# Convolution taps moved into idle stretches of VectorE, and a token scale folded into the scaling of q and k

## The chip, the cores and the metric

The kernel runs on one core of a Trainium2 chip. The metric is the device time of one execution in microseconds (us). A core has five engines that the profile names so: PE (TensorE, matmuls; its weight loads are shown as PEld), DVE (VectorE), ACT (ScalarE), POOL (GpSimd) and SP (SyncE, which here issues most of the DMAs). Each engine works through its own instructions in order and waits on semaphores for the others.

## What is computed

One layer of a hybrid encoder, with 1024 tokens of 1024 channels, all float32. The parts that matter here are the first half:

```python
h = rms_norm(x, norm1_g)
a, gate, q, k, v = split(h @ w_in)            # 512 columns each
u = a * sigmoid(gate)                         # GLU
y = depthwise_conv(u, dw_kernel) + dw_bias    # 31 taps along the tokens, for each channel
conv_out = silu(layer_norm(y))
q, k = rms_norm(q, per head), rms_norm(k, per head)    # 8 heads of 64
attn_out = neighbourhood_attention(q, k, v, rpb)       # 8 x 16 window on a 16 x 64 grid
x = x + concat(conv_out, attn_out) @ w_out
```

Then follows a SwiGLU feed-forward block of width 2816 with its own norm and residual.

## The kernel before, in words

**Matmuls.** Each float32 operand is split into a high and a low part, and each product is made of three matmuls (`mac`, lines 112 to 114). The norm's gain is applied to the transposed input, and the token scale `r1` (1 over the root mean square of a token) only after the projection, to its result in PSUM. PSUM has four banks for accumulators (`mm`), two for transposes (`tp`) and one double bank (`cv`).

**The projection stage.** One PE step is one 128-token tile of k, q or v, or one part of a GLU product, 24 matmuls of 512 columns. PE goes through: four tiles of k; the GLU of channel group 0; four tiles of k; the GLU of groups 1 to 3 (for each group two token halves `h`, for each half first the gate, part 0, then the value, part 1); eight tiles of q; eight tiles of v. Score tiles of the attention are put between the last tiles of v: score 0, v tile 6, score 1, v tile 7. Then comes the attention loop, then output projection, norm and feed-forward.

**What a step does beside PE.** `step` defers the work on a step's result by one step: it runs the callback of the step before, then one side tap (`side`). Programs are in written order; no scheduler changes it.

- `head_post` (k and q): ACT squares z by head and takes the root (`head_sq`, the result is d, line 375); DVE pumps two taps; `head_scale` takes the reciprocal (L380), multiplies it with the token scale (L381) and scales z from PSUM by it, for each head of 64 columns (L383); one more tap; the transposition on PE (`head_T`, L390) is woven in at the end of the PE step after the next, and ACT copies it to qT or kT (L395, L397).
- `gate`: DVE multiplies the accumulator with the row of token scales (L443), ACT takes the sigmoid (L444), DVE multiplies with the row again (L445), then three taps.
- `val`: DVE multiplies the accumulator with the gate into u (L451), then three taps. After the second half, u of the channel group is complete.
- v: ACT scales it and stores it by DMA; four taps are pumped.

**The convolution.** `conv_taps` is a stream of 25 VectorE operations for each of the four channel groups: a start (L314), 23 taps (L319, `acc += w * u`, u in SBUF, acc in the double PSUM bank `cv`) and an add (L324) of the seven side taps, which ACT (L341, L344) and POOL (L345) compute apart in `pa`. `pump(n)` issues the next n operations of the stream. When the stream needs a group whose u is not complete, a pump issues nothing and its turn is lost. Before score 0 is evaluated, `pump(200)` issues all that is left.

**Score evaluation.** For each score tile DVE adds the bias and finds the maximum (L624), and ACT takes the exponential (L626). The bank of a score tile is free for PE once L624 has read it.

## Time and profile before

| | before |
|---|---|
| median of 3 runs | 1070.03 us (1069.66 to 1070.52) |
| the profiled execution | 1070.39 us |
| its span, first to last instruction | 1068.6 us |
| mean granted clock of PE | 0.995 of full speed |
| DVE, ACT, POOL busy | 704.9, 451.3, 383.2 us |
| PE busy from 145 to 225 us, of 80 | 80.00 us |
| PE busy from 225 to 246 us, of 21 | 16.39 us, mean granted clock 0.84 |
| PE busy from 246 to 318 us, of 72 | 71.39 us |
| taps L319 | 92, 117.5 us |

Times in the rows of the profile are us from the start of the span unless they are marked as ns. A timeline row has start, length, engine, line, operation, out<-in, shape and count, and in brackets the idle time of the engine before it with what ended that. Lengths of successive operations can overlap a little, so the distance between two starts is what one costs in a row of them. Names such as z, zn or cv are tiles, with buffer numbers left out.

### The profile page before, as it was taken

What the parts mean: (1) busy time and instruction counts of PE and PEld (TensorE: products, weight loads), DVE (VectorE), ACT (ScalarE), POOL (GpSimd) and SP (SyncE); (2) the same over time, 40 slices, a digit from 0 to 9 for tenths busy, and PEclk for the clock granted to TensorE, in tenths of its full rate; (3) what the DMA queues carried; (4) which work ended last, traced back from release to release, by engine and by line L of the source; (5) the groups of instructions that cost most, each with busy time, mean ns of one, the idle gap of its engine ahead of it and who ended that gap; (6) DMA issues with size and microseconds to landing.
All of it is one profiled execution on the core that took longest, in us unless ns stands there. A gap on an engine that the chain in (4) does not pass through costs nothing.

```text
span 1068.6 us, 14069 instructions
## 1 busy us (share of the span) xinstructions
PE 1048.0 (98%) x5068; PEld 849.4 (79%) x5068; DVE 704.9 (66%) x1071; ACT 451.3 (42%) x987; POOL 383.2 (36%) x301
## 2 busy tenths in 40 slices
PE   7999999989999999999999999999999999999997
PEld 6788888866667888788888888888888888888886
DVE  6778997885775347766556465564655567858873
ACT  6455357725775424542322323223232344433441
POOL 0136665513562301435444554445544300002310
PEclk9999999999999999999999999999999999999999
DMA  9426781244413422132322322333232597633641
GB/s 336 158 51 221 225 251 40 75 150 137 152 62 131 164 80 82 37 107 90 128 98 84 134 99 89 109 107 109 81 129 79 179 333 276 207 98 116 216 131 41
DMA packets 68245, 144.06 MB, mean 135 GB/s; under 512 B 12496, under 2 KB 21200, under 8 KB 67536
## 3 DMA queue, kind: packets, MB, share of 16 engines
q1 hardware_dynamic: 66336, 139.95, 38.8%
q10 hardware_dynamic: 1840, 3.22, 0.9%
q8 instruction: 40, 0.66, 0.3%
q14 instruction: 29, 0.24, 0.1%
HBM read 103.99 MB, written 44.76 MB: 139 GB/s over the span
## 4 chain that ended last, share of the span: by engine, by line
PE 89%; DVE 6%; issue 1%; ACT 1%; DMA 1%; POOL 0%; SPq 0%; DVEq 0%; POOLq 0%; ACTq 0%
PE B L113 5%; PE B L114 5%; PE B L112 5%; PE D L114 4%; PE D L112 4%; PE D L113 4%; PE A L112 3%; PE A L114 3%; PE A L113 3%; DVE cv L319 3%; PE gl L114 3%; PE gl L112 3%; PE gl L113 3%; PE z L112 2%; PE z L113 2%; PE z L114 2%
## 5 line engine op out<-in xcount | busy, mean ns | idle before, releaser
L319 DVE SCALAR_TENSOR_TENSOR cv<-u,par,cv 128x1009 f32<-128x1009 f32 (+14 forms) x92 | 117.5, 1277 | 2.5
L345 POOL TENSOR_TENSOR pa<-pa,pr 128x1022 f32<-128x1022 f32 (+5 forms) x24 | 57.5, 2398 | 51.3 <-ACT pr L344 42.8
L104 ACT CAST op<-sr 128x512 fp32r<-128x512 f32 x77 | 47.7, 619 | 51.2 <-PE B2d L114 23.3
L108 DVE TENSOR_TENSOR op<-sr,op 128x512 fp32r<-128x512 f32 x77 | 57.6, 748 | 15.9 <-ACT op L104 15.8
L1036 DVE TENSOR_TENSOR g<-B,g 128x512 f32<-128x512 f32 x22 | 15.2, 691 | 79.0 <-PE B L114 79.0
L1208 POOL TENSOR_TENSOR ou<-ou,resm 128x512 f32<-128x512 f32 x8 | 13.2, 1662 | 142.9 <-DMA resm<-xd 142.9
L1045 ACT ACTIVATE D<-D 128x512 f32<-128x512 f32 x22 | 12.8, 582 | 113.1 <-DVE D L1044 113.1
L1031 DVE TENSOR_TENSOR u<-B,g 128x512 f32<-128x512 f32 x22 | 15.2, 690 | 62.5 <-PE B L114 62.5
L104 ACT CAST op<-wd 128x512 fp32r<-128x512 f32 x66 | 40.9, 619 | 31.6 <-DVE wd L1123 18.3
L108 DVE TENSOR_TENSOR op<-wd,op 128x512 fp32r<-128x512 f32 x66 | 51.7, 783 | 2.4 <-ACT op L104 0.9
L633 POOL TENSOR_SCALAR e<-e,rs 128x288 f32<-128x288 f32 (+1 forms) x64 | 34.2, 548 | 52.8 <-DVE rs L631 42.3
L889 DVE TENSOR_TENSOR ts<-gu,ts 128x512 f32<-128x512 f32 x44 | 51.0, 1159 | 0.8
L1034 ACT ACTIVATE A<-A 128x512 f32<-128x512 f32 x20 | 11.6, 582 | 76.3 <-PE A L114 76.3
L626 ACT ACTIVATE e<-e,mx 128x288 f32<-128x288 f32 (+1 forms) x64 | 36.2, 568 | 11.4 <-DVE mx L624 11.4
L624 DVE CUSTOM_DVE_ANT_0 e<-s,tab 128x288 f32<-128x288 f32 (+1 forms) x64 | 29.9, 504 | 6.7 <-PE s L611 6.4
L889 DVE TENSOR_TENSOR ts<-gu 128x512 f32<-128x512 f32 x22 | 33.5, 1524 | 0.0
L611 PE MATMUL s<-kT,qT 64*128 64x288 f32 (+1 forms) x128 | 28.1, 499 | 4.6 <-DVE mx L624 4.6
L642 PEld LDWEIGHTS p<-ident,e 128*96 128x96 f32 (+1 forms) x192 | 20.1, 133 | 15.0 <-issue 10.4
L372 ACT ACTIVATE sq<-z,r 128x64 f32<-128x64 f32 x96 | 28.6, 334 | 2.2 <-PE z L114 2.2
L642 PE MATMUL p<-ident,e 128*96 128x128 f32 (+1 forms) x192 | 27.6, 280 | 0.6 <-DVE pT L647 0.6
L658 PE MATMUL o<-pT,vw 96*64 96x128 f32 (+1 forms) x384 | 28.0, 281 | 0.0
L344 ACT ACTIVATE pr<-u,par 128x1022 f32<-128x1022 f32 (+5 forms) x24 | 27.0, 1137 | 1.6 <-ACT vs L403 1.6
(1039 smaller groups left out, 3455.0 us busy)
## 6 DMA issues: line engine op xcount, KB each, us to landing
gu<-in_gu SPq DMA_DIRECT2D x44, 512.0 KB
sr<-sd SPq DMA_DIRECT2D x77, 256.0 KB
sd<-sd SPq DMA_DIRECT2D x22, 512.0 KB
wd<-in_wd SPq DMA_DIRECT2D x44, 256.0 KB
sd<-g SPq DMA_DIRECT2D x33, 256.0 KB
x<-in_x SPq DMA_DIRECT2D x16, 512.0 KB
xd<-x SPq DMA_DIRECT2D x8, 512.0 KB
resm<-xd SPq DMA_DIRECT2D x16, 256.0 KB
```

The lines of the kernel that those rows point to most:

```text
L104: act.copy(hi, src)
L108: eng.tensor_tensor(*[w[..., sl] for w in (lo, src, hi.bitcast(F32))], OP.subtract)
L112: pe.matmul(acc, lh, rh, start=start, stop=False, skip_group_check=True)
L113: pe.matmul(acc, lh, rl, start=False, stop=False, skip_group_check=True)
L114: pe.matmul(acc, ll, rh, start=False, stop=stop, skip_group_check=True)
L319: dve.scalar_tensor_tensor(acc[:, o], uc[:, i], dwk[:, c, t:t + 1], acc[:, o], OP.mult, OP.add)
L345: pool.tensor_tensor(pa[:, o], pa[:, o], pr[:, o], OP.add)
L624: dve.tensor_tensor_reduce(out=e[:, hh], in0=ss[hh], in1=tab[rh, cb][2 * hp + hh], scale=-1.0, scalar=3.0e38, op0=OP.add, op1=OP.min, accu ...
L626: act.activation(e[:, hh], e[:, hh], AF.Exp, bias=mx, scale=-1.0, accum_out=rs[:, hh:hh + 1])
L633: pool.tensor_scalar(es[i][:, hh], es[i][:, hh], rs[:, hh:hh + 1], 1.0, op0=OP.mult, op1=OP.mult)
L642: pe.transpose(pt[:m, g * P:(g + 1) * P], es[i][:, hh, g * m:(g + 1) * m], ident)
L889: dve.tensor_tensor(o, l, r, OP.subtract)
```

## The change

In `head_scale` the separate product of the reciprocal and the token scale goes; one VectorE operation with a per-partition scalar (the token scale) and a broadcast operand (the reciprocal) scales z from PSUM. Before `head_scale`, tile 5 of k pumps three taps more and tile 1 of q two more. In `gate`, one of the three taps (for the first half of group 1, two of then four) is pumped between the two products with the row.

```diff
     def head_scale(n, t, z, sd):
         r = SM(f"r{n}{t}")
         dve.reciprocal(r, sd)
-        dve.tensor_scalar(r, r, r1[:, t:t + 1], None, op0=OP.mult)
         zn = ST(f"zn{n}{t}")
-        dve.tensor_tensor(zn.rearrange("p (h d) -> p h d", d=HD), z.rearrange("p (h d) -> p h d", d=HD),
-                          r[:, :, None].to_broadcast([P, NH, HD]), OP.mult)
+        dve.scalar_tensor_tensor(zn.rearrange("p (h d) -> p h d", d=HD), z.rearrange("p (h d) -> p h d", d=HD),
+                                 r1[:, t:t + 1], r[:, :, None].to_broadcast([P, NH, HD]), OP.mult, OP.mult)
         return zn
...
     def head_post(n, t, z):
         def f(n_taps):
             sd = head_sq(n, t, z)
-            pump(2)
+            pump(2 + {(1, 5): 3, (0, 1): 2}.get((n, t), 0))
             zn = head_scale(n, t, z, sd)
             pump(1)
...
             dve.tensor_tensor(sg, acc, row, OP.mult)
             act.activation(sg, sg, AF.Sigmoid)
+            pump(2 if (c, h) == (1, 0) else 1)
             dve.tensor_tensor(sg, sg, row, OP.mult)
-            pump(n_taps - 1)
+            pump(n_taps - 2)
```

Here n is 1 for k and 0 for q, t the tile, and n_taps is 4.

## The prediction

> **What bounds the kernel now.** I read the page first. PE is busy for 98% of the span, so only what makes PE wait or run slowly can move the end. The waits of PE come next (engine, line, what it waited for: us in total, times, longest):

> ```profile
> PE 1048.0 (98%) x5068; PEld 849.4 (79%) x5068; DVE 704.9 (66%) x1071; ACT 451.3 (42%) x987; POOL 383.2 (36%) x301
> ...
> PE z L112 <- ACT wk0h L104: 6.5, 1, 6.5
> PE s L611 <- DVE mx L624: 4.6, 1, 4.6
> ```

> The first wait is the start of the kernel, which the change doesn't touch. The second is the only other one above 1 us. PE's timeline around it (start, length, ...):

> ```profile
> 225.27 0.76 PE L611 MATMUL s<-kT,qT 64*128 64x288 f32 x4
> 225.95 0.50 PE L112 MATMUL z<-w20h,hT 128*128 128x512 f32 x1
> ...
> 231.63 0.75 PE L611 MATMUL s<-kT,qT 64*128 64x288 f32 x2
> 237.00 1.32 PE L611 MATMUL s<-kT,qT 64*128 64x288 f32 x2 [4.61 <-DVE mx L624]
> 238.25 0.79 PE L112 MATMUL z<-w20h,hT 128*128 128x512 f32 x1
> ...
> 246.17 0.76 PE L611 MATMUL s<-kT,qT 64*128 64x288 f32 x4
> ```

> Two score tiles took 225.95 - 225.27 = 0.68 us at full pace, so one takes 0.34, and the second tile of score 1 could have started at 231.63 + 0.34 = 231.97. It started at 237.00: **5.03 us lost**. It needs the PSUM bank of the first tile of score 0, and VectorE frees that bank when L624 has read it.

> There is a second loss behind the first. z(6) and its lead-in took 231.63 - 225.95 = 5.68 us, but one score tile and z(7) took 246.17 - 237.00 = 9.17 us instead of 0.34 + 5.68 = 6.02: **3.15 us lost**. The stages view says why (stretch, its length, busy time of PE, PEld, DVE, ACT, POOL, then PE's granted clock, DMA share, GB/s):

> ```profile
> 236.00:237.00 1.00, 0.01 (x1) 0.01 (x1) 1.00 (x4) 0.00 (x0) 0.00 (x0) 0.63 0.00 0
> 237.00:238.00 1.00, 1.00 (x2) 0.49 (x2) 0.32 (x2) 0.96 (x4) 0.00 (x0) 0.50 0.00 0
> ...
> 242.00:243.00 1.00, 1.00 (x4) 0.81 (x3) 0.00 (x0) 0.00 (x0) 0.00 (x0) 0.50 0.00 0
> 243.00:244.00 1.00, 1.00 (x5) 0.77 (x5) 0.00 (x0) 0.00 (x0) 0.00 (x0) 0.96 0.00 0
> ...
> 32.00:33.00 1.00, 0.35 (x2) 0.20 (x2) 0.41 (x1) 0.56 (x1) 0.75 (x1) 1.00 1.00 401
> ...
> 248.00:249.00 1.00, 0.40 (x4) 0.02 (x1) 0.56 (x1) 1.00 (x4) 0.00 (x0) 1.00 0.53 199
> ```

> The granted clock fell to half late in the wait (0.63 in its last microsecond) and stayed there until about 243.1: six microseconds of matmuls at half speed cost three. The last two rows are PE's short pauses, 0.65 and 0.60 us of idle time, and the clock stayed at 1.00 in both.

> What VectorE did before it could read the score:

> ```profile
> 201.22 0.20 DVE L380 RECIPROCAL r<-d 128x8 f32<-128x8 f32 x1 [0.86 <-ACT d L375]
> 201.46 0.23 DVE L381 TENSOR_SCALAR r<-r,r 128x8 f32<-128x8 f32 x1
> 201.79 0.69 DVE L383 TENSOR_TENSOR zn<-z,r 128x512 f32<-128x512 f32 x1
> 202.40 1.21 DVE L324 TENSOR_TENSOR u<-cv,pa 128x1024 f32<-128x1024 f32 x1
> 203.65 1.35 DVE L314 TENSOR_SCALAR cv<-u,par 128x1024 f32<-128x1024 f32 x1
> 205.03 30.21 DVE L319 SCALAR_TENSOR_TENSOR cv<-u,par,cv 128x1009 f32<-128x1009 f32 x23
> 235.34 1.22 DVE L324 TENSOR_TENSOR u<-cv,pa 128x1024 f32<-128x1024 f32 x1
> 236.49 0.45 DVE L624 CUSTOM_DVE_ANT_0 e<-s,tab 128x288 f32<-128x288 f32 x1
> ```

> From 201.22 to 236.49 VectorE never waits. It is the convolution of the last channel group, all 25 of its operations, that the score stands behind. A tap costs (235.34 - 205.03) / 23 = 1.318 us. This tail's start is set by L380, which waited for the last q head's d, so it is PE and ACT, not VectorE, that set when the tail begins. Each operation taken out of the tail therefore moves 236.49.

> **The taps.** The holes into which they go (in brackets the idle time before each):

> ```profile
> 76.56 0.20 DVE L380 RECIPROCAL r<-d 128x8 f32<-128x8 f32 x1 [5.08 <-ACT d L375]
> ...
> 93.56 1.30 DVE L445 TENSOR_TENSOR sg<-sg,rb 128x512 f32<-128x512 f32 x1 [2.11 <-ACT sg L444]
> ...
> 104.39 0.69 DVE L445 TENSOR_TENSOR sg<-sg,rb 128x512 f32<-128x512 f32 x1 [0.70 <-ACT sg L444]
> ...
> 165.69 0.20 DVE L380 RECIPROCAL r<-d 128x8 f32<-128x8 f32 x1 [2.59 <-ACT d L375]
> ```

> Head k5 gets three taps more, 3 x 1.318 = 3.95 into 5.08. Head q1 gets two, 2.64 into 2.59. Gate (1,0) gets one more; the other gates only move one of their three into the hole. That makes six. But a pump does nothing when the next channel group isn't ready, and this costs three of them. Before, group 0 had done 24 of its 25 operations when val (1,1) completed u[1]. After, the four extra taps of k5 and gate (1,0) finish group 0 inside val (1,0), and the three pumps of gate (1,1) find nothing. So at val (1,1) the stream is ahead by one, and with q1's two by **three operations**; the instruction order of the changed program has this too: after the last zn stand 22 taps and one L324.

> The tail loses one L324, the L314 and one tap: (203.65 - 202.40) + (205.03 - 203.65) + 1.318 = 3.95 us.

> Nothing on the way should stop for the fillings. The holes of the gates end with ACT's sigmoid, so the gates get shorter, not longer: 0.70 of idle time becomes part of a tap. In q1 the 0.05 by which two taps exceed the hole is covered by the shorter gates before it. Behind a late head_scale stand only head_T and, on ACT, the next head's squares. SP's queue isn't changed; ACT and POOL have the same instructions in the same order. Two adds move up, and each needs POOL's sum of the side taps:

> ```profile
> 94.71 4.86 POOL L345 TENSOR_TENSOR pa<-pa,pr 128x1018 f32<-128x1018 f32 x2 [0.40 <-ACT pr L344]
> ...
> 184.59 2.39 POOL L345 TENSOR_TENSOR pa<-pa,pr 128x1017 f32<-128x1017 f32 x1 [1.16 <-ACT pr L344]
> ```

> Group 0's add moves from 109.40 to about 100.7 (gate (1,0) ends as before at 94.8, then two taps, one product of 0.6, two taps); POOL ends at 99.57, one microsecond before. If that is missed, VectorE waits a little where three pumps are empty anyway. Group 2's add moves to about 196.2; POOL ends at 186.98.

> **The fused scaling.** In each of 16 heads L381 goes and L383 becomes a two-operation form with z in PSUM and the broadcast r in SBUF. That form with these operands is not in the trace. The nearest rows:

> ```profile
> L383 DVE TENSOR_TENSOR zn<-z,r 128x512 f32<-128x512 f32 x16 | 11.1, 692 | 1.4
> ...
> L319 DVE SCALAR_TENSOR_TENSOR cv<-u,par,cv 128x1009 f32<-128x1009 f32 x8 | 10.2, 1272 | 0.2
> ...
> L319 DVE SCALAR_TENSOR_TENSOR cv<-u,par,cv 128x1016 f32<-128x1016 f32 x8 | 10.2, 1279 | 0.2
> ...
> L260 DVE SCALAR_TENSOR_TENSOR hT<-xt,par,hT 128x256 fp32r<-128x256 f32 x16 | 7.1, 477 | 1.9 <-ACT hT L259 1.9
> ...
> L889 DVE TENSOR_TENSOR ts<-gu 128x512 f32<-128x512 f32 x22 | 33.5, 1524 | 0.0
> ```

> The taps have the same form and one operand in PSUM: 7 elements more cost 7 ns, so 512 elements should take about 1272 - 497 = 775 ns. I take 0.75, beside L383's 0.69; the ends are 0.48 (half the width) and 1.52 (the longest mean for this width). In the tail L381 saves 201.79 - 201.46 = 0.33 us and the new form gives back 0.06: 0.27 gained, between 0.54 gained and 0.50 lost. The other 15 heads gain nothing: each ends in a hole that waits for ACT or PE.

> **The sum.** L624 starts at 236.49 - 3.95 - 0.27 = 232.27. The score tile followed L624 by 237.00 - 236.49 = 0.51, so it starts at 232.78, 0.81 us after it could: of the stall of 5.03, 4.22 goes and 0.81 stays. With a pause this short, near the 0.65 and 0.60 that kept the clock, I take the clock to stay at 1.00 and all 3.15 to come back: 4.22 + 3.15 = 7.37. Bounds of that term: nothing, and 3.15.

> [...]

> Behind the stall PE runs to the end without a wait of 1 us, so I carry the 7.37 through. The profiled execution took 1070.39 (span 1068.6, and 1.79 around it): 1070.39 - 7.37 = 1063.02. The median of the three runs shown, 1070.03, is 0.36 lower, so I forecast **1062.7 us**. It can't be much better: with the stall gone altogether, 1070.03 - 5.03 - 3.15 = 1061.85.

> **The rivals.**

> *The clock falls anyway.* The pause left is longer than either of the two short pauses that the trace shows. Then only 4.22 is gained: 1065.8. Against it: the clock fell some 3.9 us into the stall. Chance 0.10.

> *The tail doesn't shrink.* The taps put in early delay the last q head by as much as they take from the tail, or a group starts later than counted. Then 1070.0, no change. For it speaks that three of six pumps are already lost; against it, that d of every q head came after a hole (0.86 before the last). Chance 0.04.

> *The new scaling makes PE wait: slower.* Its place is the woven transposition, which PE reaches just after zn:

> ```profile
> 195.87 0.69 DVE L383 TENSOR_TENSOR zn<-z,r 128x512 f32<-128x512 f32 x1
> ...
> 197.01 0.60 PE L390 MATMUL zt<-ident,zn 128*128 128x128 f32 x4
> ...
> 156.07 2.40 POOL L345 TENSOR_TENSOR pa<-pa,pr 128x1021 f32<-128x1021 f32 x1 [3.52 <-ACT pr L344]
> ...
> 157.39 1.10 DVE L381 TENSOR_SCALAR r<-r,r 128x8 f32<-128x8 f32 x1
> ```

> zn ended at 196.56, 0.45 before PE wanted it; with L381's 0.33 there is a slack of 0.78. VectorE does get held by POOL: the tiny L381 took 1.10 and ended with POOL's operation (158.49 and 158.47). If each fused scaling had to sit out a POOL operation of 2.40, PE would lose 2.40 - 0.78 = 1.62 in each of about ten heads (k5 to k7, q1 to q7): 16.2 lost and, with PE now late at the score, 8.18 of stall and clock saved: 1078.1. It decides from about 1.6 us a head. Against it: the taps of the same form with one operand in PSUM kept to 1.27 to 1.28 all through POOL's work, and POOL's side tap begins after zn in the steady heads. Chance 0.04.

> [...]

> **How the numbers follow.** Forecast 0.80, clock rival 0.10, no change 0.04, slower 0.04; I put the last 0.02 to half on unnamed small losses on each side of the limit. A measurement of this kernel can tell about 0.2%, 2.1 us, from no change; forecast and clock rival are both faster by more: faster 0.91, same 0.04, slower 0.05. The forecast's own range is 1061.8 (stall gone) to 1063.9 (the scaling at its dear end and some spread of the runs). To leave out no more than 2 in 10 the range takes in the clock rival: 1061.7 to 1066.0.

> **What would show it.** The first L624 starts near 232.3 and the second tile of score 1 near 232.8, with a PE wait on mx well under 1 us; the granted clock is 1.00 from 230 to 246; z(7) takes about 5.5 us; score 2 starts near 238.8. After the last zn come 22 taps. The holes before L445 in groups 1 to 3 are gone, the one before k5's reciprocal is about 1 us, and there is a new hole in front of val (1,1). The fused scaling takes 0.7 to 0.8. I'd be wrong if zt makes PE wait, if the clock row shows 0.50 again, or if a later stage has waits of PE that eat what the score stage gave.

## The result, and the profile after

The changed kernel takes 1063.38 us (median of 6 runs, 1062.48 to 1064.76), the kernel before 1069.94 (6 runs, 1069.44 to 1071.54): a ratio of 0.9937, 95% interval 0.9927 to 0.9948. The profiled execution took 1063.23, with a span of 1061.5 and a mean granted clock of 0.999. The forecast was 1062.7, and faster.

The waits of PE in the changed kernel. The wait on mx has shrunk from 4.6 to 0.5, and nothing new stands among the long ones:

```profile
PE z L112 <- ACT wk0h L104: 6.5, 1, 6.5
PE B L113 <- DVE S L108: 0.9, 1, 0.9
PE p L642 <- DVE pT L647: 0.6, 1, 0.6
PE s L611 <- DVE mx L624: 0.5, 1, 0.5
```

PE's timeline around the score tiles, and below it the stages view of that stretch (stretch, length, busy time of PE, PEld, DVE, ACT, POOL, granted clock, DMA share, GB/s):

```profile
224.98 0.76 PE L611 MATMUL s<-kT,qT 64*128 64x288 f32 x4
225.66 0.50 PE L112 MATMUL z<-w20h,hT 128*128 128x512 f32 x1
...
231.34 0.75 PE L611 MATMUL s<-kT,qT 64*128 64x288 f32 x2
232.55 0.75 PE L611 MATMUL s<-kT,qT 64*128 64x288 f32 x2 [0.46 <-DVE mx L624]
233.23 0.50 PE L112 MATMUL z<-w20h,hT 128*128 128x512 f32 x1
...
238.90 0.76 PE L611 MATMUL s<-kT,qT 64*128 64x288 f32 x4
```

```profile
232.00:233.00 1.00, 0.54 (x3) 0.29 (x2) 0.87 (x5) 0.41 (x1) 0.00 (x0) 1.00 0.20 78
234.00:238.00 4.00, 4.00 (x19) 3.29 (x18) 0.84 (x5) 1.46 (x5) 1.97 (x4) 1.00 0.17 66
```

z(7) now takes 238.90 - 233.23 = 5.67 us, and the clock stays at 1.00.

Executions differ in when they reach this place (the first score tile starts at 225.27 before, at 224.98 after, and between 224.62 and 226.35 in the experiments below). The yardstick from here on is therefore the **distance from the first score tile to score 2**: 246.17 - 225.27 = 20.90 before, 238.90 - 224.98 = 13.92 after, 6.98 less. From score 2 to the last matmul of the kernel it is 815.62 before and 815.58 after, so what this stretch gives is carried to the end whole. That the span is 7.1 shorter, and the time of the profiled execution 7.16, includes the 0.29 by which the first score starts sooner.

VectorE's timeline of the changed kernel, the tail:

```profile
200.93 0.20 DVE L380 RECIPROCAL r<-d 128x8 f32<-128x8 f32 x1 [1.06 <-ACT d L375]
201.23 0.75 DVE L382 SCALAR_TENSOR_TENSOR zn<-z,r,r 128x512 f32<-128x512 f32 x1
201.90 28.89 DVE L319 SCALAR_TENSOR_TENSOR cv<-u,par,cv 128x1010 f32<-128x1010 f32 x22
230.90 1.22 DVE L324 TENSOR_TENSOR u<-cv,pa 128x1024 f32<-128x1024 f32 x1
232.04 0.45 DVE L624 CUSTOM_DVE_ANT_0 e<-s,tab 128x288 f32<-128x288 f32 x1
```

22 taps and one add are left, as counted. The last L380 still starts after a hole, so ACT and PE set the tail's beginning as before. And the places where taps were put:

```profile
76.26 0.20 DVE L380 RECIPROCAL r<-d 128x8 f32<-128x8 f32 x1 [1.32 <-ACT d L375]
...
102.78 0.69 DVE L445 TENSOR_TENSOR sg<-sg,rb 128x512 f32<-128x512 f32 x1 [0.70 <-ACT sg L443]
103.58 0.69 DVE L451 TENSOR_TENSOR u<-gl,sg 128x512 f32<-128x512 f32 x1
...
117.86 0.69 DVE L442 TENSOR_TENSOR sg<-gl,rb 128x512 f32<-128x512 f32 x1 [0.31 <-PE gl L114]
...
130.53 1.52 DVE L445 TENSOR_TENSOR sg<-sg,rb 128x512 f32<-128x512 f32 x1
...
165.38 0.21 DVE L380 RECIPROCAL r<-d 128x8 f32<-128x8 f32 x1 [3.27 <-ACT d L375]
```

k5's hole went from 5.08 to 1.32. The gate at 102.78, where the pumps find nothing, keeps its 0.70. q1's hole is 3.27, longer than the 2.59 before, although two taps were put into it: VectorE now comes out of the GLU part early enough to wait for PE (117.86) and has more time left in front of q1.

### The profile page after: what moved, and what is told of

Same layout as the page of the kernel before. It is cut to its first block, busy times and chain, and to the rows that moved or that the text cites. A ratio compares the mean times of both kernels' runs of the same rounds, so it can differ in the third digit from the quotient of the medians.

```text
span 1061.5 us, 14053 instructions
## 1 busy us (share of the span) xinstructions
PE 1045.5 (98%) x5068; PEld 847.8 (80%) x5068; DVE 703.9 (66%) x1055; ACT 450.9 (42%) x987; POOL 383.8 (36%) x301
## 4 chain that ended last, share of the span: by engine, by line
PE 92%; DVE 5%; ACT 1%; issue 0%; DMA 0%; SPq 0%; DVEq 0%; ACTq 0%
PE B L113 5%; PE B L114 5%; PE B L112 5%; PE D L112 4%; PE D L114 4%; PE D L113 4%; PE A L112 4%; PE A L113 3%; PE A L114 3%; PE z L112 3%; PE z L113 3%; PE z L114 3%; PE gl L114 3%; PE gl L112 3%; PE gl L113 3%; DVE cv L319 3%
## 5 line engine op out<-in xcount | busy, mean ns | idle before, releaser
L319 DVE SCALAR_TENSOR_TENSOR cv<-u,par,cv 128x1009 f32<-128x1009 f32 (+14 forms) x92 | 117.5, 1277 | 2.4
L345 POOL TENSOR_TENSOR pa<-pa,pr 128x1022 f32<-128x1022 f32 (+5 forms) x24 | 58.0, 2415 | 50.8 <-ACT pr L344 35.2
L104 ACT CAST op<-sr 128x512 fp32r<-128x512 f32 x77 | 47.7, 619 | 50.2 <-PE B2d L114 21.3
L1036 DVE TENSOR_TENSOR g<-B,g 128x512 f32<-128x512 f32 x22 | 15.2, 690 | 79.0 <-PE B L114 79.0
L1031 DVE TENSOR_TENSOR u<-B,g 128x512 f32<-128x512 f32 x22 | 15.2, 691 | 62.0 <-PE B L114 62.0
L104 ACT CAST op<-wd 128x512 fp32r<-128x512 f32 x66 | 40.9, 619 | 33.5 <-DVE wd L1123 18.6
L889 DVE TENSOR_TENSOR ts<-gu,ts 128x512 f32<-128x512 f32 x44 | 51.0, 1159 | 0.8
L889 DVE TENSOR_TENSOR ts<-gu 128x512 f32<-128x512 f32 x22 | 33.6, 1528 | 0.0
L624 DVE CUSTOM_DVE_ANT_0 e<-s,tab 128x288 f32<-128x288 f32 (+1 forms) x64 | 29.9, 504 | 3.6 <-PE s L611 3.6
L611 PE MATMUL s<-kT,qT 64*128 64x288 f32 (+1 forms) x128 | 27.5, 495 | 0.5 <-DVE mx L624 0.5
L344 ACT ACTIVATE pr<-u,par 128x1022 f32<-128x1022 f32 (+5 forms) x24 | 27.0, 1137 | 1.6 <-ACT vs L402 1.6
```

The lines of the kernel that those rows point to most:

```text
L104: act.copy(hi, src)
L319: dve.scalar_tensor_tensor(acc[:, o], uc[:, i], dwk[:, c, t:t + 1], acc[:, o], OP.mult, OP.add)
L345: pool.tensor_tensor(pa[:, o], pa[:, o], pr[:, o], OP.add)
L624: dve.tensor_tensor_reduce(out=e[:, hh], in0=ss[hh], in1=tab[rh, cb][2 * hp + hh], scale=-1.0, scalar=3.0e38, op0=OP.add, op1=OP.min, accu ...
L889: dve.tensor_tensor(o, l, r, OP.subtract)
```

## The experiments

All times are medians; the ratio is to the kernel before on the same chip, with its 95% interval. "Distance" is that from the first score tile to score 2 in the profiled execution.

| | time, us | ratio | distance, us | clock fell |
|---|---|---|---|---|
| before | 1069.94 | | 20.90 | yes |
| changed | 1063.38 | 0.9937 (0.9927 to 0.9948) | 13.92 | no |
| e1 PE kept busy | 1067.88 | 0.9976 (0.9965 to 0.9986) | 18.18 | no |
| e2 scaling alone | 1070.00 | 0.9996 (0.9987 to 1.0004) | 19.81 | yes |
| e3 taps alone | 1064.48 | 0.9940 (0.9927 to 0.9952) | 14.13 | no |
| e4 q1's taps alone | 1066.40 | 0.9961 (0.9949 to 0.9974) | 17.02 | yes |
| e5 without k5's taps | 1063.61 | 0.9937 (0.9923 to 0.9952) | 13.91 | no |
| e6 three taps more | 1062.58 | 0.9930 (0.9917 to 0.9943) | 12.73 | no |
| e7 a tap in every q head | 1062.50 | 0.9930 (0.9916 to 0.9944) | 12.73 | no |
| e8 gates alone | 1068.89 | 0.9987 (0.9978 to 0.9996) | 19.98 | yes |
| e9 POOL beside the scaling | 1065.27 | 0.9954 (0.9940 to 0.9968) | 13.92 | no |
| e10 a pause of 1.2 | 1064.44 | 0.9948 (0.9935 to 0.9960) | 14.65 | no |
| e11 one tap in q1 | 1066.89 | 0.9965 (0.9953 to 0.9978) | 16.84 | yes |
| e12 as e4 | 1066.41 | 0.9961 (0.9946 to 0.9976) | 18.64 | yes |

### e1: the clock without the stall

The kernel before, with matmuls put into the stall whose result nobody reads:

```diff
             out.append(s)
+            if i == 1 and hh == 0:
+                f = tp("fill")
+                for _ in range(20):
+                    pe.matmul(f, hT[1][0][:, 0, :P], wn[2][0][0][:, :512], start=True, stop=True,
+                              skip_group_check=True)
```

> The kernel before, with 20 extra matmuls of 512 columns put between the two tiles of score 1; they write a spare transpose bank that nobody reads, so they only keep PE busy while it would wait for VectorE. Tail of 25 convolution operations unchanged. Theory (stall and clock are two separate losses): the second tile still starts near 237.0, the granted clock stays at 1.00, z(7) takes 5.7 us instead of 7.9, and only the clock's part comes back, 2.8 us: about 1067.1. Rival (the slow matmuls behind the stall have another cause, such as ACT and VectorE beside them, or the stall is all): no gain, 1069.9, or later than that if the extra matmuls cost time.

Measured: 1067.88. PE's timeline and the stages view of this kernel:

```profile
231.62 0.75 PE L611 MATMUL s<-kT,qT 64*128 64x288 f32 x2
...
237.07 0.75 PE L611 MATMUL s<-kT,qT 64*128 64x288 f32 x2
...
243.43 0.76 PE L611 MATMUL s<-kT,qT 64*128 64x288 f32 x4
```

```profile
232.00:237.00 5.00, 5.00 (x22) 3.68 (x20) 4.83 (x7) 0.00 (x0) 0.00 (x0) 1.00 0.03 10
237.00:243.00 6.00, 6.00 (x26) 4.64 (x26) 1.38 (x8) 2.87 (x9) 1.98 (x4) 1.00 0.12 44
```

The second tile starts at 237.07, as late as before (237.00), but the clock is 1.00 and the distance is 2.72 shorter; the medians differ by 2.35 (1070.23 before in the same comparison), where 2.8 was expected. The distance of before is 8.17 us above the shortest one seen (12.73, in e6 and e7), and this run parts that into two losses: 2.72 of clock and 5.45 of waiting.

### e2 and e3: the two parts by themselves

e2 is the kernel before with the new `head_scale`; e3 is the changed kernel with the old one.

> The kernel before with the fused scaling alone, no tap moved. Theory: the tail still has all its operations and begins 0.27 us sooner, the clock still falls: 1069.7, not to be told from before. Rival (removing 16 small operations from VectorE is worth their 16 x 0.3 us, 4.8): 1065.

> The changed kernel with the old two-step scaling: the taps alone. Theory: tail of 22 taps and one add as in the changed kernel, beginning 0.27 us later, pause of PE still short, clock 1.00: 1063.7 to 1064.0. Rival (both parts are needed, since the small pause grows over the edge of the clock): 1066 to 1067.

Measured: 1070.00, not to be told from before, and 1064.48. The cleaner reading is where the first L624 starts after the first score tile: 11.22 before and 235.64 - 224.62 = 11.02 in e2; 7.06 in the changed kernel and 233.13 - 225.86 = 7.27 in e3. The scaling is worth 0.2 us in the tail in both, and its other 15 places show no gain: e2's interval runs from 0.9987 to 1.0004. e3's median is 1.1 above that of the changed kernel, but its distance only 0.21; in its profiled execution PE's first wait, at the start of the kernel, was 7.6 instead of 6.5. e2's distance is 1.09 below that of before: 0.2 is the scaling, and most of the rest comes from the clock, which fell sooner in that execution, so that more of its slow stretch lay in the stall (the clock cases below have the times).

### e5: are k5's taps worth anything?

```diff
-            pump(2 + {(1, 5): 3, (0, 1): 2}.get((n, t), 0))
+            pump(2 + {(0, 1): 2}.get((n, t), 0))
```

> The changed kernel without the three extra taps of head k5. Theory (a channel group that ends early loses its pumps until the next is ready, so k5's taps only turn into lost pumps): group 0 ends inside val (1,1) by gate (1,0)'s extra tap alone, the tail is again 22 taps and one add, same time within 0.2 us: 1063.4. Rival (each tap put into a hole takes 1.32 us from the tail): 4.0 us of stall more, and the clock falls: about 1069.

Measured: 1063.61 and a distance of 13.91, against 1063.38 and 13.92. The tail is again 22 taps (from 202.56, 28.89 us) and one add. Three taps put into the longest hole of the stage bring nothing, since group 0 then ends early and three pumps are lost while u[1] isn't complete. The rival, 1069, is out.

### e6 and e7: is there more?

e6: `{(1, 5): 3, (0, 0): 1, (0, 1): 4}`, e7: one more tap in each of q's heads but q1.

> The changed kernel with one more tap in head q0 and two more in head q1, whose holes are 2.35 and 3.27 us long in the changed kernel's trace. Theory: the tail shrinks to 19 taps and one add, the first score is read near 228.4, before PE has finished z(6), and the stall that the changed kernel still has goes: PE's time from z(6)'s start to score 2 falls from 13.2 to 12.0 us, 1.2 less: 1062.2. Rival (the next bound is right behind: another wait of the attention's start or of a transposition takes it back): 1063.4.

> The changed kernel with one more tap in every head of q except q1. The holes there are 1.05 us, a tap is 1.32. Theory: the stall goes as with a few taps more (1.2 gained), but each of the heads q2 to q7 is 0.27 later than the one before; the transposition follows zn by 0.66, so from q4 on PE waits for zn, about 1.0 us in all: 1063.1, with waits of PE on zn in the trace. Rival 1 (zn has room enough): 1062.2, no such waits. Rival 2 (each late zn also delays ACT's next d and so builds up): later than the changed kernel by several us, 1066 or more.

Measured: 1062.58 and 1062.50. PE's timeline in e6 shows no pause at this place: both tiles of score 1 go in one piece, and 6.37 later comes score 2:

```profile
225.46 0.76 PE L611 MATMUL s<-kT,qT 64*128 64x288 f32 x4
231.82 0.76 PE L611 MATMUL s<-kT,qT 64*128 64x288 f32 x4
238.19 0.76 PE L611 MATMUL s<-kT,qT 64*128 64x288 f32 x4
```

That is 1.19 less than in the changed kernel; the times differ by 0.80, and the intervals overlap. In e7 the distance is the same, but the transposes in front of it move apart. PE's timeline in e7:

```profile
179.71 0.60 PE L389 MATMUL zt<-ident,zn 128*128 128x128 f32 x4
185.67 0.63 PE L389 MATMUL zt<-ident,zn 128*128 128x128 f32 x4
191.83 0.63 PE L389 MATMUL zt<-ident,zn 128*128 128x128 f32 x4
197.90 0.63 PE L389 MATMUL zt<-ident,zn 128*128 128x128 f32 x4
203.99 0.63 PE L389 MATMUL zt<-ident,zn 128*128 128x128 f32 x4
```

The step of 5.9 becomes 6.16, 6.07 and 6.09: from the first zt to the last it takes 42.04 us, and 41.46 before (161.47 to 202.93), so 0.58 is given back. I had expected 1.0, and waits of PE on zn in the list of waits. The list has none: the lateness is there, but in pieces too short for it (0.44 from the last matmul's start to the zt at 191.83, where 0.23 is usual). The mechanism is right and its size was too large. By these traces e6, which uses holes with room, is the better place for taps; the two times, 1062.58 and 1062.50, don't tell them apart.

### e8, e4, e12, e11, e10: from which pause on does the clock fall?

e8 is before with the gates' pumps alone; e4 and e12 are before with `pump(2 + (2 if (n, t) == (0, 1) else 0))` alone; e11 is the changed kernel with one extra tap in q1 instead of two; e10 is the changed kernel with a product that nobody uses:

```diff
+    scr = ST("scr")
+    dve.tensor_tensor(scr, u[3][0][:, :512], u[3][0][:, 512:], OP.mult)
     score_exp(0, s0)
```

> The kernel before with the taps of the gates alone (one more in gate (1,0), the other gates' third put between their products). The tail loses one add, 1.25 us, and the second tile of score 1 starts near 235.7, with PE idle for about 3.4 us instead of 4.6. Theory: this is at the edge of the clock's fall; gain 1.25 if it falls (1068.7), 4.1 if it doesn't (1065.9), and the runs may fall into two groups. Rival (the gates' shorter course by 0.7 us each also moves the tail): 5 us and more, 1064.

> The kernel before with only the two taps of head q1 added. The tail loses its first add and the start of the group, 2.63 us, so the first score is read near 233.9 and the second tile of score 1 starts near 234.4, a stall of 2.4 instead of 5.0. Theory (the clock falls only after some 3.5 to 3.9 us of idle time): clock 1.00, gain 2.6 + 2.8 = 5.4: 1064.5. Rival 1 (the clock falls in any stall of some microseconds): gain 2.6 alone, 1067.3. Rival 2 (slow matmuls in proportion to the stall): 1066.

> The same kernel as the one with only the two taps of head q1 added, once more, for a second look at its clock. Its pause is 2.0 us; in the first look the clock fell 1.7 us after PE had gone on, for one stretch of 3.4 us. Theory (stretches that run on by themselves): the fall starts at another place relative to the pause, or doesn't come; first score to score 2 between 15.4 (no fall) and 17.1. Rival (the fall follows the pause at a fixed distance): again 17.0 and a fall some 3.7 us after PE went idle.

> The changed kernel with one extra tap in q1 instead of two: the tail has 23 taps and one add, the pause of PE is about 1.8 us. Theory (the clock is judged by stretches of 3.4 us that run on by themselves, so a pause of this length falls in one of them in some executions and is cut in two in others): first score to score 2 is 15.2 us with the clock kept and about 16.9 with one stretch at half speed; the runs spread over 1064.7 to 1066.4. Rival 1 (pauses under 2 us never cost clock): all runs near 1064.7. Rival 2 (always): all near 1066.4.

> The changed kernel with one useless product of 128x512 on VectorE in front of the first score's evaluation: the pause of PE grows from 0.46 to about 1.1 us, with nothing else changed. Theory (a clock drop needs PE idle for about half of a stretch of 3.4 us, as in the run with q1's taps alone): clock 1.00, first score to score 2 takes 13.92 + 0.67 = 14.6 us, time 1064.1. Rival (any pause above those of the changed kernel costs a stretch of 3.4 us at half speed): 1065.8.

Measured: in the profiled executions the pauses of PE on mx were 3.35, 1.97, 1.97, 1.77 and 1.19 us. The clock fell in all but the last. e8's 1068.89 is the case with a fall (1068.7 expected), and its gates' shorter course doesn't move the tail. My theory for e4 (the clock falls only after some 3.5 to 3.9 us of idle time) is refuted. The stages view of e4, in which PE had gone on at 234.21:

```profile
233.00:234.00 1.00, 0.00 (x0) 0.00 (x0) 1.00 (x2) 0.00 (x0) 0.00 (x0) 1.00 0.00 0
234.00:235.00 1.00, 0.79 (x3) 0.41 (x4) 0.53 (x4) 0.75 (x3) 0.00 (x0) 1.00 0.00 0
235.00:236.00 1.00, 1.00 (x5) 0.80 (x6) 0.57 (x4) 0.97 (x3) 0.23 (x1) 0.94 0.00 0
236.00:238.00 2.00, 2.00 (x6) 1.59 (x5) 0.50 (x3) 1.15 (x4) 0.81 (x3) 0.50 0.35 131
238.00:239.00 1.00, 1.00 (x4) 0.73 (x3) 0.00 (x0) 0.00 (x0) 0.93 (x2) 0.50 0.00 0
239.00:240.00 1.00, 1.00 (x5) 0.82 (x4) 0.00 (x0) 0.00 (x0) 0.00 (x0) 0.85 0.00 0
```

The clock falls at about 235.9, 1.7 us after PE has gone on, and stays low for 3.4 us. The same program once more, e12, in which PE went on at 234.80:

```profile
234.00:235.00 1.00, 0.20 (x1) 0.20 (x2) 1.00 (x4) 0.16 (x1) 0.00 (x0) 0.91 0.00 0
235.00:236.00 1.00, 1.00 (x2) 0.29 (x2) 0.12 (x2) 1.00 (x5) 0.00 (x0) 0.50 0.00 0
...
240.00:241.00 1.00, 1.00 (x4) 0.75 (x3) 0.00 (x0) 0.00 (x0) 0.00 (x0) 0.50 0.00 0
241.00:242.00 1.00, 1.00 (x5) 0.81 (x4) 0.00 (x0) 0.00 (x0) 0.00 (x0) 0.68 0.00 0
```

Here it falls at 234.8, just as PE goes on, and stays low for 6.8 us; the distance, 18.64, lies above the 15.4 to 17.1 that I had expected, since I had counted with one stretch of 3.4 at most. So the fall doesn't follow the pause at a fixed distance: it comes 1.8 us after PE went idle in e2, 2.0 in e12, 3.3 in e8 and e11, 3.6 in e4, 3.9 before. In the six traces in which it fell, it lasted 3.4 us (e4, e11) or 6.8 (before, e2, e8, e12). In e4 and e11 PE had gone on 1.7 and 1.6 us before the fall; in the other four it went on at the fall (within 0.02 us) or after it.

This fits falls that lie on a grid of 3.4 us which doesn't begin with the pause, and the traces' records of the clock bear it out. Before, the record has the clock at full from 10.98, near the kernel's start (PE's matmuls of 512 columns start 0.43 us apart just ahead of it and 0.23 after it), to 236.26, and then at half for 6.83, or 2 x 3.413. From 10.98 to 236.26 it is 225.28 us, or 66 x 3.413. In every one of the fourteen traces this time is a whole number of 3.413 us: 65 of them in e2 and e12, 66 in before, e4, e8 and e11, and 306 to 308 in the eight in which the clock fell only after the last matmul. Laid out on this grid, PE's idle time in the stretch that ended with the fall was 1.74 us (e4), 1.77 (e11), 1.80 (e2), 1.97 (e12), 3.34 (e8) and 3.41 (before). In e10 the clock didn't fall; its pause of 1.19 lay 0.99 in one stretch and 0.20 in the next, and its five runs lie close together (1063.95 to 1065.20). Where between 0.99 and 1.74 the edge lies, no run here shows.

e11's five runs lie apart: 1064.74 and 1065.05, then 1066.89, 1067.38 and 1067.88; the theory gave 1064.7 without a fall and 1066.4 with one. e12's lie at 1065.01, 1065.40, 1067.43 and 1068.90, e4's at 1065.48, 1066.25, 1066.40, 1066.58 and 1067.91. Only the profiled execution of each has a trace, but the mean granted clock of every execution is on record, and one stretch of 3.4 us at half speed takes 0.0016 from it. It sorts these fourteen executions:

| mean granted clock | executions of e4, e11 and e12, us | the profiled ones |
|---|---|---|
| 0.998 or 0.999, as in the changed kernel | 1064.74, 1065.01, 1065.05, 1065.40, 1065.48 | none |
| 0.997 | 1066.25, 1066.40, 1066.58, 1066.89, 1067.43 | e4 (1066.25) and e11 (1066.89), low for 3.4 us |
| 0.995 or 0.996, as in the trace of before | 1067.38, 1067.88, 1067.91, 1068.90 | e12 (1068.90), low for 6.8 us |

By this one program runs with no slow stretch, with one or with two, and the spread of its times is that of its clock. That the first group are executions in which the pause was cut in two by the end of a stretch is argued, since none of them has a trace.

### e9: does POOL hold the fused scaling?

The changed kernel with work on POOL that starts as soon as d is there, its results unused:

```diff
             sd = head_sq(n, t, z)
+            if n == 0:
+                scr = ST(f"scr{t}")
+                pool.memset(scr, 1.0)
+                pool.tensor_tensor(scr[:, :8], sd, sd, OP.mult)
+                for _ in range(2):
+                    pool.tensor_tensor(scr, scr, scr, OP.mult)
```

> The changed kernel with extra work on POOL in each of the eight heads of q: as soon as d is there, a tiny product and two of 128x512 with both inputs in SBUF, whose results nobody uses. They run just while VectorE does the fused scaling. Theory (the fused scaling, with z in PSUM and one operand in SBUF, is not held by POOL): it keeps its 0.75 us and the time stays within 0.3 us of the changed kernel, 1063.4 to 1063.7. Rival (the mechanism of the prediction's slower case: it sits out the POOL operation): zn takes up to 2 us more, PE waits for it in each head of q beyond the slack of 0.66, some 5 to 10 us in all: 1068 to 1073.

Measured: the scaling keeps its length. VectorE's and POOL's timelines in e9:

```profile
155.00 0.75 DVE L382 SCALAR_TENSOR_TENSOR zn<-z,r,r 128x512 f32<-128x512 f32 x1
...
171.69 0.75 DVE L382 SCALAR_TENSOR_TENSOR zn<-z,r,r 128x512 f32<-128x512 f32 x1
...
183.56 0.75 DVE L382 SCALAR_TENSOR_TENSOR zn<-z,r,r 128x512 f32<-128x512 f32 x1
```

```profile
155.09 2.16 POOL L428 TENSOR_TENSOR scr<-scr 128x512 f32<-128x512 f32 x2
...
170.33 2.40 POOL L108 TENSOR_TENSOR w21l<-w21r,w21h 128x1024 fp32r<-128x1024 f32 x1
...
183.35 2.42 POOL L108 TENSOR_TENSOR w22l<-w22r,w22h 128x1024 fp32r<-128x1024 f32 x1
```

At 171.69 and 183.56 POOL's operation had begun before and ran on after it. The time is 1065.27, later than I expected, but not by this way: the distance is 13.92, and the delay lies ahead of it (the first score tile starts at 226.04 instead of 224.98), where POOL's split of the last v weights came late and PE waited 0.7 for it: PE's zt before that wait is 0.08 later than in the changed kernel (190.87 against 190.79), the one behind it 1.07 (197.79 against 196.72). The mechanism of the prediction's slower rival isn't there.

## Why the prediction was right, point by point

- *What bounds:* right. The wait and the slow clock behind it were two losses (e1), with them gone PE has no pause left at this place (e6), and nothing later took it back (815.6 us from score 2 to the last matmul in both).
- *Six taps, three of them lost:* right, by the 22 taps left and by e5.
- *The tail:* 3.95 + 0.27 = 4.22 forecast. From the first score tile to the first L624 it is 11.22 before and 7.06 after, so 4.16. The scaling takes 0.751, forecast 0.75, and its part is 0.2 (e2, e3) instead of 0.27.
- *What stays of the stall:* 0.81 forecast, 1.19 measured (against e6). The mis-sized term is "one takes 0.34". A score tile by itself takes 233.23 - 232.55 = 0.68, as long as two together (238.90 to 239.58): the two heads' tiles, each of 64 rows, run side by side, and in the pair their first matmuls start within 0.01 us of each other. When the second is held back, its 0.68 comes on top whole. The total loss of before wasn't touched by this, only its parts: 5.45 and 2.72 in place of my 5.03 and 3.15.
- *The clock stays at 1.00:* right, but the reason against that rival, that "the clock fell some 3.9 us into the stall", was wrong. It fell after 1.8 us in e2, and a pause of 1.8 was enough in e11; of a stretch of 3.41 us, 1.74 to 1.97 us of idle time were enough in e4, e11, e2 and e12. The changed kernel didn't put this reason to the test, since its pause was only 0.46. What made the forecast safe was the other reading, short pauses of 0.65 and 0.60 without a fall, now extended to e10's 1.19.
- *The signs:* a hole in front of val (1,1) was foretold and isn't there. VectorE began gate (1,1) 5.3 us after PE had ended it (101.40 against 96.06) and val (1,1) 2.1 us after (103.58 against 101.50), so the lost pumps shortened its lag. The holes before L445 are gone but for that of gate (1,1), which by the prediction's own count of the pumps had nothing to fill it. In three of the six gates L445 takes 1.22, 1.52 and 1.33 beside POOL, as it took 1.30 and 1.07 in two of them before; PE waited for none.
- *The sum:* 7.37 forecast for the profiled execution, 7.16 measured: 6.98 in the stretch, 0.29 at the start of the kernel (PE's first matmul with ag10l starts at 32.52 instead of 32.80, and its wait of 0.6 for it isn't there in this trace; that wait comes and goes in the other kernels too), the rest around the span. The 0.29 was not forecast and is luck. The medians differ by less, 6.56, with 5.6 to 7.8 by the interval, and the forecast of 1062.7 was 0.7 too low.

## What to carry to other kernels

Filler work that moves into an idle stretch is worth only what it takes from the place that an engine waits for: count what is left there, and look for the points where the filler's own supply is empty, since three of the six taps here were swallowed by one. A stall of PE of 1.77 us cost about as much again in clock in e11's trace (3.4 us at half speed, from 1.6 us after PE had gone on), and by the mean clock nothing in two other executions of that program; to shorten the stall to about a microsecond brought more than the time taken off it (from 4.61 to 1.19 us in e10: 3.42 off the stall, 6.25 off the distance). And before taking half the time of a pair of matmuls for one of them, look whether the pair ran side by side, as the score tiles did here (0.68 us for one, 0.68 for two).
